# A sum of the hidden halves written to another tile, and the vector engine's work of the down projections held in source order

## The chip, the cores and the metric

The kernel runs on one core of a Trainium2 chip. The metric is the device time of one execution in microseconds (us). It is a single launch, and a profile of one more execution is at hand.

## What is computed

One inference step of a two-layer encoder trunk over 1152 tokens (1024 of a prompt and 8 streams of 16), model width 1024. Each layer is a normalisation, a mixer (stick-breaking attention beside a convolution in layer 0, banded attention in layer 1), a residual, and then the part that matters here:

```python
def rmsnorm(x, g):
    xf = x.astype(jnp.float32)
    r = lax.rsqrt(jnp.mean(xf * xf, axis=-1, keepdims=True) + RMS_EPS)
    return (xf * r).astype(x.dtype) * g

def sq_relu_mlp(h, w_up, w_down):
    return jnp.square(jax.nn.relu(h @ w_up)) @ w_down
...
        xp = xp + op
        xs = xs + os_
        xp = xp + sq_relu_mlp(rmsnorm(xp, norm_ffn[layer]), w_up[layer], w_down[layer])
        xs = xs + sq_relu_mlp(rmsnorm(xs, norm_ffn[layer]), w_up[layer], w_down[layer])
```

`w_up` is 1024x4096 and `w_down` 4096x1024, all in 32-bit floats.

## The kernel before

Every product is computed as three passes over halves: `split` (lines 178 to 181) writes a value's rounded part with ScalarE (`hi`, line 180) and the remainder with VectorE (`lo`, line 181), and TensorE multiplies high by high, high by low and low by high. So each block of weights and each block of activations costs one instruction on ScalarE and one on VectorE before TensorE may read it.

Function `rest` holds the feed-forward part of a layer. Both of its matrix products use a Strassen scheme with seven products in place of eight, so sums and differences of blocks are formed around them.

**Up projection.** `unit(m)` runs 16 times (two of the 32 blocks of 128 hidden channels each time). In a unit, `k` goes over the seven products. `seven` prepares the weights of a product two ahead, `mms` issues 24 matmuls for each product (two column halves `n` of 288 tokens, four chunks, three passes), and `take` empties the PSUM bank with VectorE (lines 1417 to 1429). `done` multiplies by the row scale (line 1394), applies ReLU and square with ScalarE (1395, 1396), forms the three sums t3, t2 and b12 - b11 (1400 to 1402) once the last quarter of its column half is there, and sends the blocks to the DRAM tensor `hb_d` with transfers that GpSimd (POOL) issues (1404, 1406). A bank is used by several products in turn, so a late `take` holds up a later product.

The seventh block of a pair, `last_sum`, is formed one unit later. It is called in `unit(m)` at `k == 2` for unit m - 1 (and once more in the down projection's loop, at item 3). It subtracts t2 from the half (1, 0) of the hidden pair and writes the result over that half (line 1365), which transfer 3 of the same pair reads (line 1406); then it sends the result (1366).

**Down projection.** `todos` lists 112 items (128 in layer 1, where the last product is done in two column halves): for product `k` and block pair `j`, 24 matmuls each (12 in the halved ones), accumulated in eight banks over the 16 pairs of a chain. The loop at line 1597 does for item i: resident weight loads (`resident`), the load of item i + 4 (`load`: the hidden block from `hb_d`, and for products 3, 5 and 6 a weight block through one of three staging buffers of tag `st`), the preparation of item i + 2 (`prep`: `split_b` for activations, in one of four buffers; `split_w` for weights, with sums of weight blocks at lines 1527, 1529, 1530 and 1533), and then `item(i)`. At the end of a chain `item` adds the eight banks to the residual (line 1583). `later` holds what follows a finished quarter (squares, scaled splits, sums of squares), one entry for each item. At item 104 of layer 0, `soon` calls for the first two weight chunks of layer 1's mixer: four more staged loads with a split each, from the same three staging buffers. At the end of unit 15, `begin(0)` calls the loads of items 0 to 3 at `k == 5`, and `begin(1)` their first preparations at `k == 6`.

**What sets the order.** The instructions are not issued in source order as such. A scheduler goes over the whole program with a model of its own for the times, takes on each engine what its model has ready, earlier source lines first, and gives out buffers as they come free. So a VectorE instruction may stand far ahead of its place in the source. `tc.keep_in_program_order(ins)` adds one rule: this instruction is issued on its engine behind the instruction traced just before it on that engine. It adds no wait beyond that order. In the kernel before, it is used for the normalisation's matmuls alone (line 1446).

Of the kernel before, what the change touches and what calls it, by code (L numbers as in the profile page):

```python
# [11 lines left out]
ALU = mybir.AluOpType  # L12
# [21 lines left out]
TW = T // 2  # L34
# [6 lines left out]
def f(ap):  # L41
    return ap.bitcast(F32)
# [77 lines left out]
def tile_trunk(ctx, tc, ins, outs):  # L120
    nc = tc.nc
    ACT = nc.scalar.activation
    tt = nc.vector.tensor_tensor
# [3 lines left out]
    put = nc.gpsimd.dma_start  # L127
# [47 lines left out]
    hb_d = [dram.tile([7, NF // 2, P, TW], F32, name=f"hb_d{l}") for l in range(2)]  # L175


    def split(hi, lo, src):

        ACT(hi, src, AF.Copy)  # L180
        return tt(lo, src, f(hi), ALU.subtract)  # L181
# [168 lines left out]
    class Cat:  # L350
# [5 lines left out]
        def put(self, piece, rows, c0, n):  # L356
            if self.direct is None:
                put(cat_d[self.layer][self.p, rows, c0:c0 + n], piece[rows, :n])
                return
            at = c0  # L360
            while at < c0 + n:
                g = at // G
                m = min(c0 + n, g * G + G) - at
                hi, lo = (x[rows, self.p % 4, at - g * G:at - g * G + m] for x in self.direct[g][self.p // 4])
                split(hi, lo, piece[rows, at - c0:at - c0 + m])
                at += m
# [845 lines left out]
    def rest(layer, ks, cat, rst, mp, then, soon=None):  # L1212
# [12 lines left out]
        def pair(t, n=1024):  # L1225

            return t[:, :n].rearrange("p (a t) -> p a t", a=2)
# [129 lines left out]
        hids = []  # L1357
        tmps = [temps[n // 4][:, n % 4 * TQ:n % 4 * TQ + TQ] for n in range(8)]

        t3, t2 = extra[:, :TW], extra[:, TW:]  # L1360

        def last_sum(m):

            t4 = hids[m % 2 * 2 + 1][:, :TW]
            tt(t4, t4, t2, ALU.subtract)
            put(hb_d[layer][6, m], t4)

        def unit(m):

# [79 lines left out]
                start = 3  # L1449
            for k in range(start, 7):  # L1450
                seven(7 * m + k + 2)
                if m and k == 2:
                    last_sum(m - 1)
                if m == NF // 2 - 1 and k > 4:
                    begin(k - 5)
                for n in range(2):
                    mms(k, n, range(4))
                    if m == 0 and k == 3:
                        nx.rows[n]()
                        if n == 0:  # L1460
                            continue
                        take(k, 0)
                    if m == 0 and (k, n) == (4, 0):
                        nx.rows[2]()
                    take(k, n)
# [11 lines left out]
        a11, a21, a22, braw, bsplit, asplit, streams, bs, ws, later = ({}, {}, {}, [], [], [], {}, {}, {}, [])  # L1477
# [32 lines left out]
        def split_b(i):  # L1510
            while len(bsplit) < 4 and len(bsplit) <= i:
                bsplit.append(pair(own(("th", "xr2", "tm0", "tm1")[len(bsplit)], F32R), T))
            n = bs[i].shape[1]
            t = bsplit[i % 4][:, :, :n]
            split(t[:, 0], t[:, 1], bs[i])
            bs[i] = t

        def split_w(i):
            k, ns, j = todos[i]
            if ns == (1,):  # L1520
                ws[i] = ws[i - 16]
                return
            if k == 3 or k == 6:
                src = streams.pop(i)
            elif k == 5:
                src = streams.pop(i)
                tt(src, src, a22[j], ALU.subtract)
            elif k == 1:
                tt(a21[j], a21[j], a11[j], ALU.subtract)
                tt(a22[j], a22[j], a21[j], ALU.add)  # L1530
                src = a22[j]
            elif k == 2:
                tt(a11[j], a11[j], a22[j], ALU.add)
                src = a11[j]
            else:
                src = a11[j] if k == 0 else a21[j]
            if k == 6 and layer == 1:
                w = pair(place(j // 2, j % 2, F32R, f"wk{name}"))
            elif k == 6:
                if j < 8:  # L1540
                    tag = ("sl8", "sl9", "sl10", "sl11", "lo0", "lo1", "lo2", "xr3")[j]
                    asplit.append(pair(own(tag, F32R)))
                w = asplit[j % 8]
            elif i % 6 < 4:
                w = sp.tile([P, 2, 512], F32R, "hl", f"hl_wd{layer}{i}")
            else:
                w = pair(few[i % 6 - 4])
            split(w[:, 0], w[:, 1], src)
            ws[i] = w

        def prep(i):
            if i < len(todos):
                split_b(i)
                split_w(i)

        def begin(n):

            if n == 0:
                for i in range(4):
                    load(i)  # L1560
            else:
                prep(0)
                prep(1)
# [3 lines left out]
        def item(i):  # L1567
            k, ns, j = todos[i]
            first = any(k == chain[0] for chain in chains) and j == 0
            b, w = bs.pop(i), ws[i]  # L1570
            for m in range(4):
                for n in ns:
                    if first:
                        banks[m, n] = bank(f"pd{layer}{k}{m}{n}")
                    ps = banks[m, n][:, :TQ]
                    for s, (a, h) in enumerate(SPLIT):
                        mm(ps, w[:, a, m * P:m * P + P], b[:, h, (n - ns[0]) * TQ:(n - ns[0]) * TQ + TQ],  # L1577
                           start=first and s == 0, stop=j == NF // 2 - 1 and s == 2,
                           skip_group_check=not any(k == chain[0] for chain in chains))
                    if j == NF // 2 - 1:  # L1580
                        for e, half in out[k]:
                            xs = x[4 * e + m][:, half * TW + n * TQ:half * TW + n * TQ + TQ]
                            tt(xs, xs, ps, ALU.add)
            if j == NF // 2 - 1 and k in final:
                later.extend(then(x, *final[k], None if len(ns) > 1 else ns[0], sq))

# [10 lines left out]
        for i in range(len(todos)):  # L1597
            if i == 3:
                last_sum(NF // 2 - 1)
            if 2 <= i < 18:  # L1600
                resident("a11", i - 2)
            if 14 <= i < 30:
                resident("a21", i - 14)
            if 16 <= i < 32:
                resident("a22", i - 16)
            c = {n: m for m, n in enumerate((6, 7, 8, 9, 40, 41, 42, 43))}.get(i)
            if c is not None:
                x[c] = own(f"sl{c}", F32)
                dma(x[c], xr_d[layer][c])
            load(i + 4)  # L1610
            prep(i + 2)
            item(i)
            if i == 104 and soon:
                soon()
            for _ in range(1 + (len(later) > len(todos) - i)):
                if later:
                    later.pop(0)()
# [220 lines left out]
```

## Time and profile before

| | |
|---|---|
| median of 3 runs (lowest to highest) | 2860.11 us (2855.12 to 2863.78) |
| profiled execution, its own time | 2856.45 us |
| its span, first to last instruction | 2854.7 us |
| mean granted TensorE clock | 0.985 |
| TensorE matmuls (PE) | 2708.8 us busy, 95% |
| VectorE (DVE) | 2141.5 us busy, 75% |
| ScalarE (ACT) | 1376.3 us busy, 48% |
| GpSimd (POOL) | 330.5 us busy, 12% |

Up projections are the matmuls of line 1388, down projections those of line 1577. In a row of the timeline the columns are start, duration, engine, line, operation, what is written <- what is read, size and count; in brackets stands the idle time of the engine before it and what released it. In a row of waits the three numbers are the total in us, how often, and the longest. In a table of windows each engine has its busy time and number of instructions, then come the granted TensorE clock, the share of the DMA engines and GB/s. Names leave buffer numbers out: `um` and `pd` are PSUM banks of the up and the down projection, `hl_wd`, `hl_wc` and the like split weights, `st_wd` and `st_wc` staged ones; `th`, `xr` and `tm` also name the buffers of split activations in the down projection. A busy matmul row counts the modelled, overlapping duration; the pace is read from the starts.

### The profile page before, as it was taken

How to read it: one execution, taken by the hardware profiler on the slowest of the kernel's cores; microseconds unless marked ns; L12 is line 12 of the kernel's file. 1: busy time of each engine (PE TensorE's matmuls, PEld its weight loads, DVE VectorE, ACT ScalarE, POOL GpSimd, SP SyncE). 2: the span in 40 equal slices, each digit the busy share in tenths (PEclk: the TensorE clock that was granted, in tenths of full speed). 3: DMA queues.
4: the chain of work that ended last, by engine and by line, in shares of the span. 5: the costliest groups of instructions: out<-in, count | busy, mean ns of one | idle time of the engine just before them, and what ended most of it. 6: DMA issues, size and time to landing. Idle time of an engine off the chain costs nothing.

```text
span 2854.7 us, 50855 instructions
## 1 busy us (share of the span) xinstructions
PE 2708.8 (95%) x19362; PEld 2594.2 (91%) x19362; DVE 2141.5 (75%) x4201; ACT 1376.3 (48%) x2898; POOL 330.5 (12%) x599
## 2 busy tenths in 40 slices
PE   8988988899999998999999999998999999989998
PEld 8987876799999998999999999997999999989998
DVE  8999999988677768557467777778787676685566
ACT  5344446665444443445355555556554444434343
POOL 1000101031111110000011111110321111100001
PEclk9999998999999999999999999999999999999999
DMA  4434346444333386336444444446543333873354
GB/s 154 131 96 133 107 134 201 147 165 139 128 132 132 137 288 222 109 96 212 139 142 139 143 137 135 136 132 222 173 146 130 124 137 131 283 232 96 93 173 139
DMA packets 177813, 431.31 MB, mean 151 GB/s; under 512 B 26480, under 2 KB 54320, under 8 KB 175520
## 3 DMA queue, kind: packets, MB, share of 16 engines
q1 hardware_dynamic: 140304, 296.77, 33.1%
q0 software_dynamic: 37120, 131.27, 13.5%
q8 instruction: 152, 2.49, 0.4%
q14 instruction: 93, 0.76, 0.1%
q10 hardware_dynamic: 144, 0.02, 0.0%
HBM read 297.98 MB, written 117.34 MB: 145 GB/s over the span
## 4 chain that ended last, share of the span: by engine, by line
PE 51%; DVE 24%; DMA 9%; issue 8%; ACT 7%; POOL 0%; SPq 0%; DVEq 0%; POOLq 0%; ACTq 0%
PE pd L1577 21%; PE psc L220 10%; PE um L1388 6%; DMA hb_d<-hdm 4%; DVE y L669 4%; DVE kp L843 2%; PE avc L401 2%; PE tpc L389 2%; DVE sg L845 1%; PE f L220 1%; PE psoa L220 1%; DVE hdm L1394 1%; DVE hl_m L181 1%; DMA st_wd<-in_w_down_dram 1%; DVE wla L181 1%
## 5 line engine op out<-in xcount | busy, mean ns | idle before, releaser
L220 PE MATMUL psc<-h,hl_wc 128*128 128x384 f32 x1728 | 327.2, 339 | 0.0
L220 PEld LDWEIGHTS psc<-h,hl_wc 128*128 128x128 f32 x1728 | 296.9, 188 | 13.3 <-issue 10.9
L1388 PE MATMUL um<-sl,hl_m 128*128 128x288 f32 x1548 | 244.7, 299 | 11.2 <-DVE hdm L1423 10.0
L1388 PEld LDWEIGHTS um<-sl,hl_m 128*128 128x128 f32 x1548 | 219.7, 190 | 14.6 <-ACT hdm L1396 8.2
L1577 PE MATMUL pd<-tm,hl_wd 128*128 128x288 f32 x1536 | 210.4, 295 | 4.9 <-DVE tm L181 3.9
L1577 PEld LDWEIGHTS pd<-tm,hl_wd 128*128 128x128 f32 x1536 | 205.2, 189 | 6.8 <-DVE tm L181 5.0
L669 DVE SCALAR_TENSOR_TENSOR y<-u,dw,y 128x1024 f32<-128x1024 f32 (+1 forms) x232 | 176.5, 809 | 0.4
L220 PE MATMUL psp<-h,hl_wi 128*128 128x384 f32 x864 | 168.3, 343 | 0.2 <-ACT kps L892 0.2
L220 PEld LDWEIGHTS psp<-h,hl_wi 128*128 128x128 f32 x864 | 149.2, 190 | 6.4 <-issue 4.9
L1395 ACT ACTIVATE hdm<-hdm 128x288 f32<-128x288 f32 x192 | 84.3, 439 | 138.8 <-DVE hdm L1394 138.8
L180 ACT ACTIVATE hl_m<-xr 128x512 fp32r<-128x512 f32 x132 | 81.0, 622 | 136.2 <-DVE xr L1338 117.7
L1388 PE MATMUL um<-sl,hl 128*128 128x288 f32 x756 | 124.3, 304 | 15.4 <-DVE hdm L1423 15.0
L181 DVE TENSOR_TENSOR tm<-xr,tm 128x576 fp32r<-128x576 f32 (+1 forms) x120 | 85.3, 714 | 70.0 <-ACT tm L180 70.0
L180 ACT ACTIVATE tm<-xr 128x576 fp32r<-128x576 f32 (+1 forms) x120 | 77.6, 647 | 119.2 <-PE pd L1577 98.2
L1388 PEld LDWEIGHTS um<-sl,hl 128*128 128x128 f32 x756 | 109.9, 194 | 18.7 <-DVE hdm L1423 16.9
L181 DVE TENSOR_TENSOR hl_m<-xr,hl_m 128x512 fp32r<-128x512 f32 x132 | 92.3, 700 | 44.7 <-ACT hl_m L180 44.7
L1104 ACT ACTIVATE s<-s,mxc 128x640 f32<-128x640 f32 (+4 forms) x128 | 88.9, 694 | 60.1 <-DVE mxc L1101 58.5
L1577 PE MATMUL pd<-th,hl_wd 128*128 128x288 f32 x768 | 107.8, 295 | 2.3 <-DVE hdm L1429 2.2
L1577 PE MATMUL pd<-tm,hl 128*128 128x288 f32 x768 | 105.9, 295 | 1.2 <-DVE tm L181 1.2
L1577 PE MATMUL pd<-xr,hl_wd 128*128 128x288 f32 x768 | 106.9, 295 | 0.0
L1577 PEld LDWEIGHTS pd<-th,hl_wd 128*128 128x128 f32 x768 | 103.5, 189 | 3.2 <-DVE hdm L1429 2.7
L1577 PEld LDWEIGHTS pd<-tm,hl 128*128 128x128 f32 x768 | 103.3, 188 | 2.1 <-DVE tm L181 2.1
(527 smaller groups left out, 6809.6 us busy)
## 6 DMA issues: line engine op xcount, KB each, us to landing
xr<-hb_d SPq DMA_DIRECT2D x208, 288.0 KB, 2.9
hb_d<-hdm POOLq DMA_DIRECT2D x128, 288.0 KB, 3.0
xr<-in_w_up_dram SPq DMA_DIRECT2D x64, 512.0 KB, 4.4
st_wd<-in_w_down_dram SPq DMA_DIRECT2D x96, 256.0 KB, 3.5
hb_d<-t POOLq DMA_DIRECT2D x64, 288.0 KB, 2.4
wm<-in_w_down_dram SPq DMA_DIRECT2D x64, 256.0 KB, 4.7
st_wc<-in_w_in_c_dram SPq DMA_DIRECT2D x48, 256.0 KB, 2.9
xm_d<-xo POOLq DMA_DIRECT2D x16, 576.0 KB, 3.5
```

The source lines that it names most:

```text
L180: ACT(hi, src, AF.Copy)
L181: return tt(lo, src, f(hi), ALU.subtract)
L220: mm(ps()[:, :G], hl[:, a, at:at + P], act[g][k // 4][b][:, k % 4, :], start=n == 0, stop=n == len(todo) - 1)
L389: nc.tensor.transpose(tp[:, c0 + q * P:c0 + (q + 1) * P], blocks.get(j, tile_q), ident)
L401: mm(st["av"][:, o0:o0 + n], vs[:, j, i].rearrange("p a d -> p (a d)"), src[:, c0:c0 + n], start=st["done"] == 0, stop=st["done"] == nmm - 1)
L669: stt(src if j == CW - 1 else dst, src, wj, dst, ALU.mult, ALU.add)
L843: nc.vector.tensor_tensor_scan(keep[:, 0:n][:, ::-1], keep[:, 0:n][:, ::-1], ones[:, 0:1].to_broadcast([P, n]), 1.0, ALU.mult, ALU.mult)
L845: tt(w[:, 0:n - 1], w[:, 0:n - 1], keep[:, 1:n], ALU.mult)
L1104: ACT(s[:, :n], s[:, :n], AF.Exp, bias=mx, scale=-1.0, accum_out=tot)
L1388: mm(banks[b, n][:, :TQ], w[:, a, c * P:c * P + P], combo(key, c)[:, h, n * TQ:n * TQ + TQ], start=k < 3 and c == 0 and i == 0, stop=c == ...
L1395: ACT(y, y, AF.Relu)
L1577: mm(ps, w[:, a, m * P:m * P + P], b[:, h, (n - ns[0]) * TQ:(n - ns[0]) * TQ + TQ], start=first and s == 0, stop=j == NF // 2 - 1 and s == ...
```

## The change

It has two parts. First, `last_sum` writes its result to t3 in place of the hidden half itself, the transfer reads t3, and the call stands at `k == 1` of the next unit, with the instruction kept in source order. Second, in the down projections every VectorE instruction that belongs to an item (the splits of `split_b` and `split_w`, the sums of weight blocks, the additions to the residual) is kept in source order, and the difference a21 - a11 (line 1529) leaves `split_w` and is done at items 18 to 33, between `prep(i + 2)` and `item(i)`. The VectorE instructions of `later`, of `soon` and of the up projection's `take` and `done` are not marked.

```diff
         t3, t2 = extra[:, :TW], extra[:, TW:]
+        pinned = tc.keep_in_program_order
 
         def last_sum(m):
 
-            t4 = hids[m % 2 * 2 + 1][:, :TW]
-            tt(t4, t4, t2, ALU.subtract)
-            put(hb_d[layer][6, m], t4)
+            pinned(tt(t3, hids[m % 2 * 2 + 1][:, :TW], t2, ALU.subtract))
+            put(hb_d[layer][6, m], t3)
...
                 seven(7 * m + k + 2)
-                if m and k == 2:
+                if m and k == 1:
                     last_sum(m - 1)
...
             t = bsplit[i % 4][:, :, :n]
-            split(t[:, 0], t[:, 1], bs[i])
+            pinned(split(t[:, 0], t[:, 1], bs[i]))
             bs[i] = t
...
             elif k == 5:
                 src = streams.pop(i)
-                tt(src, src, a22[j], ALU.subtract)
+                pinned(tt(src, src, a22[j], ALU.subtract))
             elif k == 1:
-                tt(a21[j], a21[j], a11[j], ALU.subtract)
-                tt(a22[j], a22[j], a21[j], ALU.add)
+                pinned(tt(a22[j], a22[j], a21[j], ALU.add))
                 src = a22[j]
             elif k == 2:
-                tt(a11[j], a11[j], a22[j], ALU.add)
+                pinned(tt(a11[j], a11[j], a22[j], ALU.add))
                 src = a11[j]
...
-            split(w[:, 0], w[:, 1], src)
+            pinned(split(w[:, 0], w[:, 1], src))
             ws[i] = w
...
-                            tt(xs, xs, ps, ALU.add)
+                            pinned(tt(xs, xs, ps, ALU.add))
...
             load(i + 4)
             prep(i + 2)
+            if 18 <= i < 34:
+                pinned(tt(a21[i - 18], a21[i - 18], a11[i - 18], ALU.subtract))
             item(i)
```

## Prediction

> **What bounds the kernel now.** I read the page first, then the waits of VectorE and TensorE, then windows of the two stages that the change touches, then timelines inside them.
>
> ```profile
> span 2854.7 us, 50855 instructions
> PE 2708.8 (95%) x19362; PEld 2594.2 (91%) x19362; DVE 2141.5 (75%) x4201; ACT 1376.3 (48%) x2898; POOL 330.5 (12%) x599
> DVE hdm L1365 <- DMA hb_d<-hdm: 100.1, 32, 5.9
> PE um L1388 <- DVE hdm L1423: 25.1, 17, 2.3
> PE pd L1577 <- DVE sl L1583: 13.9, 3, 6.1
> PE pd L1577 <- DVE tm L181: 5.0, 7, 1.2
> 676.00:1031.80 355.80, 341.30 (x2529) 337.72 (x2528) 252.56 (x494) 164.88 (x375) 56.90 (x105) 1.00 0.41 144
> 2111.00:2464.70 353.70, 341.57 (x2519) 339.22 (x2518) 250.88 (x490) 164.06 (x373) 56.85 (x105) 0.99 0.42 144
> 1363.33 3.36 PE L1577 MATMUL pd<-th,lo 128*128 128x288 f32 x24
> 1366.53 3.36 PE L1577 MATMUL pd<-xr,lo 128*128 128x288 f32 x24
> ```
>
> TensorE bounds the kernel; only its holes can be won. Undisturbed it starts 24 matmuls of 288 columns in 1366.53 - 1363.33 = 3.20 us, 0.1333 each. The two windows hold the up projections without their first units: 2529 and 2519 matmuls would take 337.2 and 335.9 us, so 18.6 + 17.8 = 36.4 us are lost there. VectorE is not the bound by its share, but it stands still 32 times, once in each unit, 3.1 us on average, in front of the last sum (L1365) until a transfer has read the half that the sum overwrites. One unit shows how that reaches TensorE:
>
> ```profile
> 752.79 0.54 POOL L1406 DMA_DIRECT2D hb_d<-hdm  x1 [1.66 <-ACT tm L1415]
> 759.52 0.76 DVE L1365 TENSOR_TENSOR hdm<-hdm,t 128x576 f32<-128x576 f32 x1 [5.90 <-DMA hb_d<-hdm]
> 767.00 2.53 PE L1388 MATMUL um<-sl,hl 128*128 128x288 f32 x9 [2.25 <-DVE hdm L1423]
> 733.10 0.76 DVE L1365 TENSOR_TENSOR hdm<-hdm,t 128x576 f32<-128x576 f32 x1 [2.20 <-DMA hb_d<-hdm]
> 741.01 1.22 PEld L1388 LDWEIGHTS um<-sl,hl_m 128*128 128x128 f32 x9 [0.34 <-ACT hdm L1396]
> ```
>
> Where VectorE stood 5.90 us, the bank for product 6 came 2.25 us late; where it stood 2.20 us, TensorE lost about 0.3 us. A unit of 168 matmuls has 22.4 us. The first window holds 2529 / 168 = 15.1 units with 252.56 us of VectorE, 16.8 for each, so without the stand it has room; with it, and with short waits for ScalarE's half of each split, it has little.
>
> **Part one: the last sum into t3.** The overwritten operand was the only reason to wait for transfer 3. Nothing is added: one instruction of 0.76 us and one transfer stay. The new place adds one wait: t3 must have been read by its own transfer (L1404). That is issued 4.4 us before transfer 3 (748.42 against 752.79); the landings are those of the t2 and t3 transfers in layer 0.
>
> ```profile
> 748.42 0.54 POOL L1404 DMA_DIRECT2D hb_d<-t  x1 [3.90 <-DVE t L1400]
> 752.07 0.43 ACT L1396 ACTIVATE hdm<-hdm 128x288 f32<-128x288 f32 x1
> DMA to landing us min/median/max: 2.4/2.4/4.5
> ```
>
> Even at the longest landing (4.5 us) t3 is free at 752.9, 0.4 us after the square that the sum needs. The next writer of t3 is L1400 one unit later, some 17 us after the new transfer's issue: no wait there. POOL's later transfers move forward with the sum. The pin puts it behind a weight split that has run long before, and so holds nothing. Ends: all 36.4 us (TensorE gapless), or half, 18, if the scheduler still leaves it in a poor place. I take 33, near the upper end, since the unit with a stand of 2.2 us already lost almost nothing.
>
> Of those losses a part is clock: after the hole at 764.9 to 767.0 the granted clock is 0.50.
>
> ```profile
> 767.50:770.00 2.50, 2.50 (x12) 2.50 (x12) 1.78 (x4) 2.17 (x5) 0.00 (x0) 0.50 0.31 118
> 1094.50:1098.00 3.50, 3.42 (x15) 3.45 (x16) 3.50 (x9) 0.00 (x0) 0.00 (x0) 0.52 0.90 284
> ```
>
> The Trainium skill ("TensorE: Matmul & The Clock Gate", Part 1) has the clock halved only after an idle window of about 3.4 us. By that, holes of at most 2.3 us cost their 25.1 us alone, the rest of the 36.4 has another cause and stays, and the forecast comes out 8 us longer, 2824. This trace does not agree: 2.25 us were enough, so I give that no chance of its own.
>
> **Part two: down projections in source order.** What the order of the scheduler costs now:
>
> ```profile
> 1093.39 0.68 DVE L1530 TENSOR_TENSOR lo<-lo,wm 128x512 f32<-128x512 f32 x1
> 1093.99 3.00 DVE L1583 TENSOR_TENSOR sl<-sl,pd 128x288 f32<-128x288 f32 x8
> 1094.58 4.88 PE L1577 MATMUL pd<-th,hl 128*128 128x288 f32 x24 [6.13 <-DVE sl L1583]
> ```
>
> At the first chain's end VectorE forms sums of weights (L1530 here) that are due 16 items later, and empties the banks after them. Pinned, the eight additions (3.00 / 8 = 0.375 us each) follow each bank's end, every 0.40 us, and the next item finds its banks. That takes away the 13.9 us of waits for L1583 (one of 6.1 in each layer and a third), and 3.5 x 0.48 = 1.7 us of half clock after each long one: 17. The waits for L181 (5.0 us) have the same cause except at the start: 4. The sums, undone there, fall into items 16 to 47: neighbours overlap by 0.08 us (0.68 long, 0.60 apart, at 1093.39), so VectorE has then 0.67 + 0.61 for the two splits and 0.61 for a sum, 1.9 us per item, 2.5 where a second sum falls, against 3.20: covered by TensorE.
>
> The pins cost something at three joins, where unpinned work stands ahead of them.
>
> The first is the start. Items 0 and 1 are now prepared behind L1402 of unit 15; before, weight 0 was split at 1025.54.
>
> ```profile
> 1025.54 0.69 DVE L181 TENSOR_TENSOR hl_wd<-st_wd,hl_wd 128x512 fp32r<-128x512 f32 x1 [1.15 <-ACT hl_wd L180]
> 1030.08 0.45 DVE L1426 TENSOR_TENSOR hdm<-um,tm 128x288 f32<-128x288 f32 x1
> 1032.65 0.75 DVE L1400 TENSOR_TENSOR t<-hdm,hdm 128x576 f32<-128x576 f32 x1
> 1034.35 0.75 DVE L1402 TENSOR_TENSOR hdm<-hdm 128x576 f32<-128x576 f32 x1
> 1035.53 0.67 PE L1577 MATMUL pd<-th,hl_wd 128*128 128x288 f32 x3 [0.77 <-DVE hdm L1429]
> 1043.40 0.40 PE L1577 MATMUL pd<-tm,hl_wd 128*128 128x288 f32 x1 [0.78 <-ACT tm L180]
> ```
>
> From L1426 to L1402's end are 5.0 us, 4.0 without the weight split (0.69) and the addition (0.45) that stood between; item 0's two splits add 1.4. Product 6's 24 matmuls cover 3.2 of these 5.4 to 6.4 us: TensorE waits 2.2 to 3.2, and half clock may add 1.5. The two holes shown (1.55 us) go. Net 0.6 to 3.2 a layer; I take 1.5, so 3.
>
> The second is `soon` in layer 0. Its four splits are not pinned, but item 107's split is pinned behind the last of them.
>
> ```profile
> 1361.58 0.33 SPq L187 DMA_DIRECT2D st_wc<-in_w_in_c_dram  x1
> 1368.21 0.93 SPq L187 DMA_DIRECT2D st_wc<-in_w_in_c_dram  x2
> 1370.09 2.36 SPq L187 DMA_DIRECT2D st_wd<-in_w_down_dram  x2
> 1367.49 0.69 DVE L181 TENSOR_TENSOR hl_wc<-st_wc,hl_wc 128x512 fp32r<-128x512 f32 x1 [2.07 <-ACT hl_wc L180]
> 1371.40 0.69 DVE L181 TENSOR_TENSOR hl_wc<-st_wc,hl_wc 128x512 fp32r<-128x512 f32 x1 [1.34 <-ACT hl_wc L180]
> ```
>
> SP's order shows staging buffers given out in source order: the four st_wc, then items 109 and on. Now items 107 and 108 hold two of the three buffers until their splits, which wait for the four; so the four pass one after another through one buffer. One pass, issue to split's end, is 1372.09 - 1368.21 = 3.9 us, or 1368.18 - 1361.58 = 6.6 at worst. It begins when item 106 is split, about 2.2 us after item 103 starts (then its activation buffer comes free; two VectorE splits of 1.4 behind one of ScalarE). With 4.5 a pass: 2.2 + 18 + 1.4 = 21.6 us, where four items cover 12.8. TensorE stands 8.8 us (6.4 to 17.2 by the ends). SP's loads for 109 on wait too, but land before they are due. I take 9.
>
> The third is layer 1's last product, 16 items of 12 matmuls. Its weight splits ran ahead; pinned, they fall into it.
>
> ```profile
> 2786.86 0.69 DVE L181 TENSOR_TENSOR wkm<-st_wd,wkm 128x512 fp32r<-128x512 f32 x1 [1.22 <-ACT wkm L180]
> 2790.38 0.75 DVE L1657 TENSOR_TENSOR accfin<-accfin,t 128x576 f32<-128x576 f32 x1
> 2797.79 0.62 DVE L276 TENSOR_SCALAR accfin<-ident,v_fin 96x96 f32<-96x96 f32 x3
> 2803.73 2.28 DVE L1719 SCALAR_TENSOR_TENSOR sl<-sl,norms,rfin 128x576 f32<-128x576 f32 x3
> ```
>
> An item has 12 x 0.1333 = 1.6 us. VectorE, by starts: 15 pairs of splits (0.61 and, for half an activation, 0.37) 14.7; four sums of squares at 0.67, 2.7; two normalisations at 1.2 (the diagonal, 0.62, and five small steps, put as long) 2.4; eight scalings at 2.28 / 3 = 0.76, 6.1. That is 25.9 us against 15 items' 24.0. I take 2, between 0 (TensorE's own extra work covers it) and 6 (waits of the in-order queue come on top).
>
> **Sum.** Against the profiled execution's own 2856.45 (0.13% under the median 2860.11): -33 - 17 - 4 + 3 + 9 + 2 = -40, so 2816. Less than 0.3%, 8.6 us, can't be told from no change.
>
> **Rivals.** (a) *The joins cost nothing* (buffers are given out otherwise, the first splits float): -54, 2802. SP's order above speaks against it. (b) *The last sum still waits*, now for t3's transfer or in a poor place: 18 in place of 33, 2831. The maximum landing of 4.5 us speaks for a wait of 0.4 at most. (c) *Slower: the staging loop.* With splits pinned, a staging buffer is freed only at its item's turn, and the loop of three buffers (landing, two splits of 1.4, up to one item of waiting) must stay under three items, 9.6 us. At the median landing it is 3.5 + 1.4 + 3.2 = 8.1.
>
> ```profile
> DMA to landing us min/median/max: 2.5/3.5/9.2
> ```
>
> At a mean landing over 5.0 it binds; the 96 streamed items must slip 0.5 us each, a landing of 6.5, to take back the 40 and cost 8.6 more: 2865. (d) *No change*: the holes only move, since TensorE's next limit lies right behind; 2856; against it stand the 16.8 us of VectorE in a unit of 22.4.
>
> **Numbers.** Forecast 0.52, (a) 0.20, (b) 0.13, (c) 0.08, (d) 0.07. Faster by over 0.3%: the first three, 0.85; the same 0.07; slower 0.08. The range runs from (a) with all of the 36.4, 2799, to (b) with the second join at its worse end, 2839, and 3 us beyond either, as runs of one kernel spread (2855.12 to 2863.78): 2796 to 2842. It leaves out (c) and (d).
>
> **What would show it.** L1365 with under 1 us of idle time before it; PE's waits for L1423 nearly gone and the two windows near 338 us; no wait of 6 us for L1583; new PE holes at the first down matmul (2 to 3 us), at item 107 of layer 0 (9 us) and small ones after item 98 of layer 1. The forecast is wrong if the mixer between, whose order the scheduler makes anew, shifts by more than some us, or if VectorE is seen waiting for st_wd at its pins.

## The result, and the profile after

The changed kernel took 2830.38 us (median of 4 runs, 2823.68 to 2831.08) beside 2857.61 us for the kernel before on the same chip (2850.0 to 2863.78): a ratio of 0.9901, with a 95% interval of 0.9871 to 0.993. That is inside the range given. The profiled execution took 2830.25 us, 26.2 under the 2856.45 of before, where the forecast had 40.

Line numbers below the last sum's own shift a little between the kernels. In the changed one, the down projection's matmul is line 1576 (1577 before), the addition to the residual line 1582 (1583 before), and the difference a21 - a11 of the down weights line 1612; the up projection's matmul stays at 1388 and the last sum at 1365.

A ledger by stage says more than the total. Each stage is taken from the first matmul of its line to the first matmul of the next stage's line (the down projections to their own last matmul's end), in us of each kernel's profiled execution. The last column is the ratio to the kernel before, from the timed runs.

| kernel | up, layer 0 | down, layer 0 | up, layer 1 | down, layer 1 | span | ratio |
|---|---|---|---|---|---|---|
| before | 387.4 | 370.1 | 385.3 | 378.0 | 2854.7 | 1 |
| changed | 378.1 | 369.4 | 375.9 | 369.9 | 2828.5 | 0.9901 |
| part one alone (`e1_sum_alone`) | 375.2 | 371.6 | 373.6 | 376.3 | 2832.1 | 0.9927 |
| part two alone (`e2_pins_alone`) | 385.0 | 370.6 | 383.2 | 369.6 | 2839.8 | 0.9963 |
| `e7_dest_only` | 374.8 | 372.0 | 374.8 | 376.4 | 2832.4 | 0.9937 |
| `e8_in_place` | 382.9 | 370.4 | 383.7 | 369.9 | 2840.7 | 0.9975 |
| `e3_late_soon` | 373.6 | 360.1 | 375.0 | 369.3 | 2809.8 | 0.9865 |
| `e4_late_s1` | 365.9 | 368.7 | 366.1 | 368.8 | 2807.0 | 0.9827 |
| `e5_both` | 364.6 | 360.6 | 366.1 | 370.8 | 2798.9 | 0.9807 |
| `e6_fewer_pins` | 378.2 | 357.1 | 373.5 | 360.5 | 2802.8 | 0.9834 |
| `e10_additions_only` | 376.7 | 370.4 | 372.2 | 374.6 | 2826.9 | 0.9941 |
| `e11_weight_sums` | 376.6 | 359.0 | 374.9 | 360.5 | 2805.5 | 0.9824 |
| `e9_best` | 364.6 | 356.6 | 365.6 | 359.6 | 2779.0 | 0.9759 |

The mixer between the layers took 675.7 to 678.5 us in all of them, and what lies ahead of the first up projection 642.8 to 647.9: the time moved in the four stages named. Between kernels that have the same source in a stage it differs by up to 4.6 us (the up projections of the changed kernel, of `e3_late_soon`, `e6_fewer_pins`, `e10_additions_only` and `e11_weight_sums`), so a difference of a few us in one stage is not argued from without a row that shows it. The spans are those of one execution each; in `e8_in_place` and `e10_additions_only` it was the shortest of the timed ones, 4.4 and 7.2 us under their medians.

Of the changed kernel, the page's head, its waits, and the windows of the up projections, which end at the first down matmul as the ones before did and are as long within 1.2 us:

```profile
span 2828.5 us, 50713 instructions
PE 2705.3 (96%) x19362; PEld 2592.1 (92%) x19362; DVE 2146.1 (76%) x4201; ACT 1380.5 (49%) x2898; POOL 329.5 (12%) x599
DVE s1m L1336 <- DMA xr<-in_w_up_dram: 79.4, 28, 4.2
PE um L1388 <- DVE hdm L1423: 12.6, 18, 1.3
PE pd L1576 <- DVE tm L181: 6.6, 3, 5.8
667.00:1022.70 355.70, 348.12 (x2597) 345.16 (x2596) 261.04 (x507) 174.12 (x395) 57.77 (x107) 1.00 0.43 150
2094.00:2446.50 352.50, 347.44 (x2594) 344.90 (x2594) 261.14 (x507) 174.16 (x395) 57.78 (x107) 1.00 0.43 150
```

Three things are to be seen. VectorE's stand of 100.1 us before the last sum has left the list, and a new one of 79.4 us is at its head: L1336, the sum s1 of two blocks of the *up* weights, waits 28 times (2.8 us each) for the load of those weights. TensorE's waits for L1423 are halved, not gone. In about the same time TensorE starts 2597 and 2594 matmuls where it started 2529 and 2519; at the prediction's 0.1333 us the windows still lose 355.7 - 346.2 = 9.5 and 352.5 - 345.8 = 6.7 us.

What L1365 itself now waits for, in the view of that one line:

```profile
  ACT hdm L1396: 13.3, 18
  DMA hb_d<-t: 3.0, 2
```

That is 16.3 us in 32 calls, 0.5 each, as the prediction asked for (under 1 us). But this is what became of the room, in the timeline of one unit:

```profile
750.60 2.42 SPq L1323 DMA_DIRECT2D xr<-in_w_up_dram  x2
752.58 0.75 DVE L1365 TENSOR_TENSOR t<-hdm,t 128x576 f32<-128x576 f32 x1
754.70 0.69 DVE L1338 TENSOR_TENSOR xr<-s1m,xr 128x512 f32<-128x512 f32 x1
759.10 0.69 DVE L1336 TENSOR_TENSOR s1m<-xr 128x512 f32<-128x512 f32 x1 [3.33 <-DMA xr<-in_w_up_dram]
764.48 1.45 PE L1388 MATMUL um<-sl,hl 128*128 128x288 f32 x9 [0.20 <-DVE hdm L1423]
```

The last sum runs at 752.58 without a stand, and 2.4 us after its end VectorE stands all the same, 3.33 us, in front of s1. Each unit forms s1 (L1336), then a21 - a11 (L1337), then a11 (L1338) from it. Product 2 of this unit starts at 751.4, so the L1338 at 754.70 is already the next unit's, and the s1 at 759.10 that of the unit after: the scheduler has put it more than a unit (22 us) ahead of its place in the source. VectorE comes to it at 755.77, 3.1 us after the second of its two loads was issued (753.02 less 0.33), and the load lands 3.33 us later.

In the down projections the profile has both sides of part two. The waits for L1583 are gone. At `soon` in layer 0, the timelines of SP, VectorE and TensorE:

```profile
1358.08 12.39 SPq L187 DMA_DIRECT2D st_wc<-in_w_in_c_dram  x4
1373.96 0.33 SPq L187 DMA_DIRECT2D st_wd<-in_w_down_dram  x1
1361.68 0.69 DVE L181 TENSOR_TENSOR hl_wc<-st_wc,hl_wc 128x512 fp32r<-128x512 f32 x1 [3.63 <-ACT hl_wc L180]
1365.49 0.69 DVE L181 TENSOR_TENSOR hl_wc<-st_wc,hl_wc 128x512 fp32r<-128x512 f32 x1 [3.12 <-ACT hl_wc L180]
1369.42 0.69 DVE L181 TENSOR_TENSOR hl_wc<-st_wc,hl_wc 128x512 fp32r<-128x512 f32 x1 [3.24 <-ACT hl_wc L180]
1373.23 0.69 DVE L181 TENSOR_TENSOR hl_wc<-st_wc,hl_wc 128x512 fp32r<-128x512 f32 x1 [3.12 <-ACT hl_wc L180]
1364.40 4.42 PE L1576 MATMUL pd<-tm,sl 128*128 128x288 f32 x32
1374.65 4.33 PE L1576 MATMUL pd<-tm,sl 128*128 128x288 f32 x16 [5.82 <-DVE tm L181]
1378.78 3.75 PE L1576 MATMUL pd<-th,lo 128*128 128x288 f32 x24
1374.70:1378.20 3.50, 3.50 (x14) 3.40 (x15) 3.01 (x5) 0.63 (x1) 0.00 (x0) 0.50 0.81 246
```

The four mixer chunks pass one after another through one staging buffer: of their four loads each but the first is issued within 0.03 us of the end of the split before it (as that of st_wd at 1373.96, behind the last), a split every 3.8 to 3.9 us, and TensorE stands at item 107. The 32 matmuls from 1364.40 end about 1368.67, so 5.98 us are lost; the next 16 take 4.13 us in place of 2.13, at a granted clock of 0.50, and the 24 after them 3.59 in place of 3.20. Together 8.4 us.

### The profile page after: what moved, and what is told of

It reads as the page before. It is cut to its first block, busy times and chain, and to the rows that moved or that the text cites. A ratio compares the mean times of both kernels' runs of the same rounds, so it can differ in the third digit from the quotient of the medians.

```text
span 2828.5 us, 50713 instructions
## 1 busy us (share of the span) xinstructions
PE 2705.3 (96%) x19362; PEld 2592.1 (92%) x19362; DVE 2146.1 (76%) x4201; ACT 1380.5 (49%) x2898; POOL 329.5 (12%) x599
## 4 chain that ended last, share of the span: by engine, by line
PE 51%; DVE 24%; DMA 10%; ACT 8%; issue 6%; SPq 0%; POOL 0%; DVEq 0%; ACTq 0%; POOLq 0%
PE pd L1576 19%; PE psc L220 10%; PE um L1388 9%; DMA xr<-in_w_up_dram 4%; DVE y L669 4%; DMA st_wd<-in_w_down_dram 3%; DVE kp L843 3%; PE avc L401 2%; DVE hl_m L181 2%; PE tpc L389 2%; DVE sg L845 1%; PE psoa L220 1%; PE f L220 1%; DMA wm<-in_w_down_dram 1%; DVE wla L181 1%
## 5 line engine op out<-in xcount | busy, mean ns | idle before, releaser
L1576 PEld LDWEIGHTS pd<-xr,hl_wd 128*128 128x128 f32 x768 | 103.7, 189 | 1.2 <-DVE hl_wd L181 0.8
```

## The experiments

**Each part alone.** The kernel before with part one, and the changed kernel with the last sum as it was:

```diff
 # e1_sum_alone, against before
+        pinned = tc.keep_in_program_order
...
-            tt(t4, t4, t2, ALU.subtract)
-            put(hb_d[layer][6, m], t4)
+            pinned(tt(t3, hids[m % 2 * 2 + 1][:, :TW], t2, ALU.subtract))
+            put(hb_d[layer][6, m], t3)
...
-                if m and k == 2:
+                if m and k == 1:
 # e2_pins_alone, against the changed kernel: the same lines, all but the first, the other way round
```

> The first part alone: the last sum goes to t3, one product earlier in the source and kept in source order; the down projections are as before. Theory (the two parts act in different stages and add): the two up projections come from 387.6 and 385.5 us to 378 and 376, the down projections stay at 370 and 378, the whole is 17 to 20 us shorter than before, 2838 beside 2857. Rival (the parts need each other: a shorter up projection only brings the down projections' stalls forward): less than 10 us shorter. Either way VectorE stands still in front of the sum of weight blocks s1 until the up weights have landed, some 2.8 us a unit.

Measured: 2833.8 us, ratio 0.9927 (0.9912 to 0.9942), 19.6 us under the 2853.36 of the kernel before.

> The second part alone: the down projections' VectorE work in source order, the last sum as before. Theory: the up projections stay at 386 to 388 us with 3.1 us of waiting a unit for the transfer; in the down projections the two holes of 6 us at the first chain's end go, and a hole of 6 us at item 107 of layer 0 comes, so that they take 369 and 370 us: 8 to 10 us shorter than before, 2848. Rival: the hole at the first chain's end goes only if the up projection ends in the new order; then the down projections stay at 370 and 378.

Measured: 2841.82 us, ratio 0.9963 (0.9952 to 0.9974), 11.5 us under. The waits of VectorE in the two, and of TensorE in the second:

```profile
DVE s1m L1336 <- DMA xr<-in_w_up_dram: 80.7, 28, 4.8
```

```profile
DVE hdm L1366 <- DMA hb_d<-hdm: 106.4, 32, 6.2
PE um L1389 <- DVE hdm L1424: 24.6, 19, 2.3
PE pd L1577 <- DVE th L181: 5.8, 2, 2.9
```

Part one brings its gain in the up projections and the new stand with it, without part two. Part two brings its gain in the second down projection (378.0 to 369.6; the first stays at 370, with one hole gone and one new) and leaves TensorE's waits for the emptied banks (24.6 us) where they were. The parts add up (19.6 + 11.5 = 31 against 1 - 0.9901 of 2857.6, which is 28, with 20 to 37 in its interval), and the larger is part one's. The last row is a surprise that is needed below: with the old last sum in the last unit, the first item waits 2.9 us a layer for its split; in the changed kernel it is 1.05 in both layers.

**What of part one does it: the destination, the place or the pin?**

```diff
 # e7_dest_only, against before: t3 as the destination, no pin, still after product 2
-            t4 = hids[m % 2 * 2 + 1][:, :TW]
-            tt(t4, t4, t2, ALU.subtract)
-            put(hb_d[layer][6, m], t4)
+            tt(t3, hids[m % 2 * 2 + 1][:, :TW], t2, ALU.subtract)
+            put(hb_d[layer][6, m], t3)
 # e8_in_place, against the changed kernel: pin and place kept, written over the operand
-            pinned(tt(t3, hids[m % 2 * 2 + 1][:, :TW], t2, ALU.subtract))
-            put(hb_d[layer][6, m], t3)
+            t4 = hids[m % 2 * 2 + 1][:, :TW]
+            pinned(tt(t4, t4, t2, ALU.subtract))
+            put(hb_d[layer][6, m], t4)
```

> The kernel before with one edit: the last sum is written to t3 and t3 is what the transfer reads; it stands after product 2 as before and is not pinned. Theory: the destination does it all, since the overwritten operand was the only reason to wait: no stand before L1365, up projections 374 to 376 us each as with the whole first part (375.2 and 373.6), ratio 0.992 to 0.994, about 2834 us. Rival: the place and the pin matter: unpinned, the scheduler puts the sum where the splits wait behind it, the up projections keep half of the loss (380 to 382 each), about 2845 us.

Measured: 2834.01 us, ratio 0.9937 (0.9918 to 0.9955); up projections 374.8 and 374.8.

> The changed kernel, but the last sum overwrites its operand as before and sends that; it stays pinned after product 1. Theory: the wait for the transfer that reads the operand is back and, since the sum comes one product earlier, longer than before: VectorE stands 100 to 150 us before L1365, the up projections take 385 to 400 us each, the down projections as in the changed kernel; 2840 to 2870 us. Rival: the pin alone brings the gain, because the order of VectorE is what counted: VectorE stands under 60 us, up projections under 382 each, about 2835 us.

Measured: 2846.86 us, ratio 0.9975 (0.9963 to 0.9987); up projections 382.9 and 383.7. VectorE's first wait:

```profile
DVE hdm L1366 <- DMA hb_d<-hdm: 106.8, 32, 5.4
```

The destination does all of part one. With it alone the up projections are as short as with the whole part, and without it pin and place leave the stand at 106.8 us. Nor do they bring anything: `e2_pins_alone` is the same kernel without them and has a ratio of 0.9963, lower than the 0.9975 here. That the earlier place would make the stand much longer was expected and did not come: 106.8 us are as much as the 106.4 of `e2_pins_alone`, and the number for the up projections (385 to 400) was too high.

**The new wait.** In the changed kernel, the two sums at the head of a unit's weights are called at a place of their own and pinned there: product 4 of the unit before.

```diff
 # e4_late_s1, against the changed kernel
+        early_s1 = {}
+
+        def sums(m, pin=lambda ins: ins):
+            a1, a2 = raws[m]
+            s1 = early_s1[m] = sp.tile([P, 512], F32, "st", f"s1{name}{m}")
+            pin(tt(s1, a2[:, :512], a2[:, 512:], ALU.add))
+            pin(tt(a2[:, :512], a2[:, :512], a1[:, :512], ALU.subtract))
...
-                tt(s1, a21, a22, ALU.add)
-                tt(a21, a21, a11, ALU.subtract)
+                if m not in early_s1:
+                    sums(m)
+                s1 = ups["s1"] = early_s1[m]
...
+                if 0 < m < NF // 2 - 1 and k == 4:
+                    sums(m + 1, pinned)
```

> The changed kernel with the two sums of up-weight blocks that wait for a landing (s1 and a21 - a11) called at product 4 of the unit before, each kept in source order, so that they stand behind the additions that empty product 3's banks. Theory (VectorE's wait for the up weights has taken the place of the wait removed, and holds up the additions behind it): the 79 us of waits for the up weights go, the 12.6 us of TensorE's waits for the emptying of product 4's bank too, and the up projections come to 369 to 371 us each, 12 to 16 us in all under the changed kernel. Rival (VectorE's work in a row between products 2 and 4 is itself too long): the waits for the load go, the holes at product 6 stay at 0.7 us or more, and the gain is under 4 us.

Measured: 2806.44 us, ratio 0.9827 (0.9807 to 0.9847). VectorE's longest sum of waits, then what s1 (L1330 here) waits for in all, and one unit of the timeline (L1346 is L1338 of the other kernels):

```profile
DVE tm L181 <- ACT tm L180: 80.6, 52, 4.9
  DMA xr<-in_w_up_dram: 2.3, 2
751.70 0.68 DVE L1330 TENSOR_TENSOR s1m<-xr 128x512 f32<-128x512 f32 x1
754.11 0.69 DVE L1346 TENSOR_TENSOR xr<-s1m,xr 128x512 f32<-128x512 f32 x1
```

The sum now stands 2.4 us ahead of the one that uses it, not a unit ahead, and its 79.4 us of waiting are 2.3. It does not stand where the expectation put it, behind product 3's additions: its pin holds it behind a weight split that itself runs ahead, and it comes between the additions of product 1.

The up projections fall by another 12.2 and 9.8 us, more than expected (369 to 371 was; 365.9 and 366.1 came), and TensorE has no wait left there for an emptied bank. So the stand before s1 held back what part one could give: with it gone, the up projections are 40.7 us shorter than before, with it 18.7. (That is the least of the seven kernels that have the new destination and the old s1; the other six have 21.0 to 24.1.)

**The hole at item 107.** `soon` is called at the last item of the down projection:

```diff
 # e3_late_soon, against the changed kernel
-            if i == 104 and soon:
+            if i == len(todos) - 1 and soon:
```

> The changed kernel with the first two weight chunks of the next mixer called for at the last item of the down projection of layer 0 in place of item 104, so that none of this stage's pinned work stands behind their splits. Theory (the four splits stand ahead of item 107 and pass one after another through one staging buffer): the hole of 5.8 us at item 107 goes, the down projection of layer 0 takes 361 to 363 us in place of 369.4, the mixer after it starts without a new wait over 1 us, and the whole is 6 to 8 us shorter than the changed kernel. Rival (the hole comes from the loads' landing, not from the order): the chunks are now late at the mixer's start and the hole moves there, no gain.

Measured: 2815.46 us, ratio 0.9865 (0.985 to 0.9879). The hole is gone, the first down projection 360.1 us (369.4), and nothing came in its place in the mixer. Its first up projection, which the edit doesn't touch, also came out 4.5 us shorter; with the other repair beside it (next run) no such difference shows.

```diff
 # e5_both, against the changed kernel: the edits of e4_late_s1 and e3_late_soon
```

> The changed kernel with both repairs at once: the sums s1 and a21 - a11 called and pinned at product 4 of the unit before, and `soon` called at the last item. Alone, by their profiles, the first left the up projections at 365.9 and 366.1 us (378.1 and 375.9 in the changed kernel) and the second the down projections of layer 0 at 360.1 (369.4). Theory: the two holes lie in different stages and add: up projections 365 to 367 each, first down projections 359 to 362, TensorE shows neither a wait of about 6 us before item 107 nor waits of VectorE for the up weights; ratio to the kernel before 0.979 to 0.981, about 2796 to 2800 us. Rival: the gain of the late `soon` was half a gift of the scheduler's other order (its up projections were also 4.5 us shorter in layer 0), then the two don't add and the ratio stays at 0.982 or above.

Measured: 2798.42 us, ratio 0.9807 (0.9787 to 0.9828). The two holes add, as two different stages should.

**Which pins does part two need?** Three kernels keep one kind or two of the pins of the down projections:

```diff
 # e6_fewer_pins, against the changed kernel: the splits free, sums and additions pinned
-            pinned(split(t[:, 0], t[:, 1], bs[i]))
+            split(t[:, 0], t[:, 1], bs[i])
...
-            pinned(split(w[:, 0], w[:, 1], src))
+            split(w[:, 0], w[:, 1], src)
 # e10_additions_only, against e6_fewer_pins: the sums of lines 1527 to 1532 and 1612 free too, for instance
-                pinned(tt(a21[i - 18], a21[i - 18], a11[i - 18], ALU.subtract))
+                tt(a21[i - 18], a21[i - 18], a11[i - 18], ALU.subtract)
 # e11_weight_sums, against e6_fewer_pins: the additions free, the sums pinned
-                            pinned(tt(xs, xs, ps, ALU.add))
+                            tt(xs, xs, ps, ALU.add)
```

> The changed kernel without the pins of the weight splits and the activation splits; the sums of the weights and the eight residual additions stay pinned. Theory: the gain of part two comes from the additions and the sums alone, and the splits pay the price: with them free the four splits of `soon` need not pass through one buffer, so the hole before item 107 of layer 0 and the small waits for VectorE's splits in the staging loop go; first down projections 361 to 364 us (369.4 in the changed kernel), the second 367 to 369, 6 to 9 us under the changed kernel, ratio about 0.987. Rival: the splits need their pins; free, they are put behind other work again, TensorE's waits for L181 come back (5 us or more in all), and the time is that of the changed kernel or up to 5 us above.

Measured: 2803.32 us, ratio 0.9834 (0.9806 to 0.9862). Better than expected: both down projections gain (12.3 and 9.4 us), and TensorE is busy in all but 0.2 us of the first:

```profile
1024.00:1381.00 357.00, 356.80 (x2691) 356.59 (x2691) 233.55 (x378) 156.64 (x254) 10.23 (x19) 1.00 0.57 182
```

> The changed kernel with only the eight residual additions of each product pinned in the down projections; the sums of the weights and the splits are not. Theory: the wait of about 6 us was the order of the additions behind sums that are due much later, so pinning the additions alone takes it away: no wait of TensorE for L1582 over 1 us, down projections 357 to 362 us each, the time of the kernel without pinned splits, ratio 0.982 to 0.985. Rival: free sums are still put ahead of the additions at the first chain's end, since a pinned addition keeps its place behind them only if they were called later; then the waits of about 6 us stay, down projections 366 to 372 each, ratio 0.988 to 0.992.

Measured: 2835.88 us, ratio 0.9941 (0.9922 to 0.9961). The theory fell; the rival's mechanism came, at a ratio above its 0.988 to 0.992. The wait is back, and VectorE's timeline before it shows why:

```profile
PE pd L1576 <- DVE sl L1582: 14.1, 3, 6.8
1080.57 0.68 DVE L1612 TENSOR_TENSOR wm<-wm,wm 128x512 f32<-128x512 f32 x1
1081.17 1.29 DVE L1529 TENSOR_TENSOR lo<-lo,wm 128x512 f32<-128x512 f32 x2
1082.38 3.00 DVE L1582 TENSOR_TENSOR sl<-sl,pd 128x288 f32<-128x288 f32 x8
1082.97 3.46 PE L1576 MATMUL pd<-th,hl 128*128 128x288 f32 x13 [6.80 <-DVE sl L1582]
```

Line 1612 is called from item 18 on, and yet it runs ahead of the additions that close item 15: the pin of an addition keeps it behind the instruction traced before it, and keeps nothing from being put in front of the pair. The one to hold is the instruction that runs ahead.

> The changed kernel with only the sums of the weight blocks pinned in the down projections; the splits and the eight residual additions of each product are not. With only the additions pinned the down projections took 370.4 and 374.6 us and the wait of 6 to 7 us for L1582 stayed; with both pinned they took 357.1 and 360.5. Theory: the sums held at their own items are the whole of part two's gain, since nothing else stands ahead of the additions: no wait for L1582 over 1 us, down projections 356 to 362 us each, ratio 0.982 to 0.985. Rival: the additions need their pins as well, since a free addition can be put behind the splits of the next items: waits for L1582 of 1 to 6 us, down projections 364 to 372 each, ratio 0.986 or above.

Measured: 2807.06 us, ratio 0.9824 (0.98 to 0.9847); down projections 359.0 and 360.5. The sums' pins, with a21 - a11 at its new place, are the whole gain: the new place without the pins is `e10_additions_only`, and the pins without the new place were not run. The additions need none, and the pins of the splits only cost.

**The version that the runs point to:** the sums of the up weights late (`e4_late_s1`) and no pin on the splits (`e6_fewer_pins`).

```diff
 # e9_best, against the changed kernel: the edits of e4_late_s1 and e6_fewer_pins
```

> The changed kernel with the sums s1 and a21 - a11 called and pinned at product 4 of the unit before, and without the pins of the splits. Alone the first left the up projections at 365.9 and 366.1 us, the second the down projections at 357.1 and 360.5. Theory: the two act in different stages and add: up projections 365 to 367 each, down projections 357 to 361 each, about 20 us under the first repair alone: 2784 to 2790 us, ratio 0.975 to 0.978. Rival: the free splits of the down projections' first items now compete with the sums pinned in the last unit, and the start of each down projection loses 2 to 5 us: ratio 0.979 or above.

Measured: 2784.18 us, ratio 0.9759 (0.9739 to 0.9779), 70 us under the kernel before in the same call (2854.34) and far below the changed one. The windows of its four stages:

```profile
643.30:1007.90 364.60, 362.32 (x2714) 360.27 (x2713) 292.57 (x564) 193.27 (x417) 62.05 (x111) 1.00 0.44 155
1007.90:1364.60 356.70, 356.70 (x2693) 356.70 (x2691) 234.04 (x378) 157.39 (x254) 10.29 (x20) 1.00 0.56 181
2041.80:2407.40 365.60, 362.55 (x2714) 360.27 (x2713) 293.35 (x564) 193.25 (x417) 62.70 (x112) 1.00 0.44 154
2407.40:2767.00 359.60, 359.60 (x2720) 359.26 (x2719) 238.40 (x422) 153.99 (x267) 11.28 (x21) 1.00 0.53 170
```

TensorE is busy from end to end of both down projections and lacks 2 to 3 us in each up projection. Little is left to be won there by order.

## Why the prediction was right, and where its sum was not

The mechanism of both parts was as forecast: the stand before the last sum was the overwritten operand's (`e7_dest_only`, `e8_in_place`), and the waits for L1583 came from sums of weights put ahead of the additions (`e10_additions_only`, `e11_weight_sums`). The sizes, term by term:

**Last sum and up projections: -33 forecast, -18.7 measured.** This is the term that was mis-sized, and its 14.3 us are about as much as the 13.8 between forecast and profiled execution. Its lower end (18) is what came, though not for the reason given there: the last sum's own place cost nothing (0.5 us of waiting a unit). The step that failed is "so without the stand it has room". It counted VectorE's work but did not ask what is late next. The next was the load of the up weights: in the kernel before, the stand had covered it (s1 waited 2.0 us there, in 2 calls), so no large row of that profile warned of it; the loads and s1 stood in the same timelines and could have been set against each other, once the last sum's stand was thought away.

The prediction's own two windows, taken from and to the same matmuls, show the size. They lasted 355.8 and 353.6 us before, 345.6 and 341.1 in the changed kernel (22.7 less), and 335.6 and 334.0 in `e4_late_s1` (39.8 less), so the new wait held back 17.1. The stretches ahead of them, which the prediction left out, grew by 3.9 us in the changed kernel; in `e3_late_soon`, with the same source, they did not. That the 39.8 are above the upper end of 36.4 is a matter of pace: in `e4_late_s1` every unit after the first takes 22.3 to 22.4 us, 0.1327 a matmul and not 0.1333, and there were some 5050 of them.

**Down projections: -21 for the waits, +14 for the joins, -7 in all; measured -8.7** (the rounded stages of the ledger give 8.8). Split by items, both layers together, in us against the kernel before; `e6_fewer_pins` has the pins that work without those that cost:

| items | forecast | changed | `e6_fewer_pins` |
|---|---|---|---|
| 0 to 12, with the start | +3 | -2.8 | -8.3 |
| 13 to 16, the first chain's end | -21 | -17.0 | -21.0 |
| 17 to 95 | 0 | -1.4 | -1.4 |
| the rest of layer 0, with `soon` | +9 | +8.4 | +0.1 |
| the rest of layer 1 | +2 | +4.2 | +0.3 |

The -21 for the waits was right in size: with the splits free it came whole. The pins of the splits cost 21.7 us (the difference of the last two columns), not 14: some 5.5 at the start, 4.0 at items 13 to 16, which the forecast put at nothing, 8.3 with `soon` and 3.9 at the end of layer 1. The start came out shorter all the same, because the kernel before lost 8.3 us there (6.5 against `e11_weight_sums`, whose splits are free too), where the prediction took off two holes of 1.55 us a layer. The net agrees partly by luck, since a start that was 5.8 us better than forecast pays for what the chain's end and layer 1's end cost more.

- *Join 2, `soon`: +9 forecast, 8.4 in the profile.* The place, the item, the buffer and the pass (3.8 to 3.9 us; 4.5 taken) were as forecast; the clock at 0.50 behind the hole was not in the sum and made up for the shorter passes, so the agreement to 0.6 us is in part luck. Moving `soon` took out 9.3 us of the stage.
- *Join 1, the start: +1.5 a layer forecast, a gain measured.* In the changed kernel, in layer 0:

```profile
1022.71 1.10 PE L1576 MATMUL pd<-th,hl_wd 128*128 128x288 f32 x7
1023.39 0.75 DVE L1402 TENSOR_TENSOR hdm<-hdm 128x576 f32<-128x576 f32 x1
1024.05 0.75 DVE L181 TENSOR_TENSOR th<-xr,th 128x576 fp32r<-128x576 f32 x1
1024.86 2.13 PE L1576 MATMUL pd<-th,hl_wd 128*128 128x288 f32 x14 [1.05 <-DVE th L181]
1024.90:1027.90 3.00, 3.00 (x23) 3.00 (x23) 2.96 (x6) 0.82 (x2) 0.53 (x1) 1.00 1.05 400
```

  VectorE's order is the one forecast (the split behind L1402), but TensorE starts item 0 on the high halves, which need no VectorE, and so covers 0.93 us more; the hole of 1.05 us leaves the clock at 1.00, so the 1.5 us of half clock did not come. In the kernel before, items 0 to 2 took 1043.40 - 1031.80 = 11.6 us for 9.6 us of matmuls; here they take 11.1. Two steps failed: an item was taken to need all of its halves before it starts, and the last unit's own stand was left in although part one takes it away. With that stand (`e2_pins_alone`; 4.74 us in the last unit of layer 0, and another 1.76 in which VectorE waits there for a late square of ScalarE) the hole is 2.9 us behind the same 0.93, so the forecast's 2.2 to 3.2 would have been near by two errors.
- *Join 3, the end of layer 1, +2 forecast, +4.2 measured:* waits for splits show there, under 1 us each, 1.6 us in all, while the 1.7 us that the kernel before waited there for L1583 are gone. The rest of the 4.2 was not traced.
- *Put at nothing:* small holes at items 13 to 15, the last of the first product with streamed weights, 2.0 us a layer more than in `e6_fewer_pins`. VectorE's pinned split waits 2.4 to 3.2 us there for ScalarE's, which waits for the staged load, and the load is issued as the split before it ends (1063.25 behind 1063.22). That is rival (c), the staging loop, right in kind and far off in size. It is also the last sign that the prediction named against itself, VectorE waiting for st_wd at its pins, by way of ScalarE.

**The rivals.** Of (b), half of the up projections' loss stayed and the time was 2830 against its 2831, but not by its mechanism; a time that agrees proves no cause. Of (a), the condition was that the first splits float; `e6_fewer_pins` made it true and came to 2803 against its 2802, by other terms: -21.0 in the up projections for -33, and -30.4 in the down projections for -21.

## What to carry to other kernels

Before a wait is priced as a gain, think it away in the timeline and look for the next thing that the same engine will meet; a wait that now covers another leaves it hardly a row. Pin the instruction that runs ahead (here, sums due many items later), not what it delays and not the splits around it: a pinned instruction behind an unpinned transfer waits for that transfer's buffer too. And read a change by stage, and a stage by items: a net that agrees can be terms that are off both ways.

## What was not expected of the hardware

The length of a hole does not tell what TensorE's clock does behind it. In the kernel before, the four longest holes of the up projections are 2.23 to 2.25 us long. Behind two of them, those that end at 767.00 and 2223.53, the granted clock is 0.50; behind the other two, at 910.73 and 2341.99, it stays at 1.00. The holes of 2.91 and 2.90 us at the start of the second down projection part the same way: half clock in `e2_pins_alone` (hole's end at 2461.82), full in `e8_in_place` (2462.96). Windows of 3.41 us around the holes at 767.00 and 910.73, then around these two:

```profile
763.34:766.75 3.41, 1.41 (x11) 1.18 (x9) 2.27 (x6) 2.18 (x5) 0.00 (x0) 1.00 0.00 0
766.75:770.16 3.41, 3.16 (x13) 3.16 (x14) 2.66 (x6) 2.19 (x5) 0.68 (x2) 0.50 0.22 87
906.70:910.11 3.41, 1.80 (x14) 1.56 (x12) 2.27 (x5) 1.90 (x5) 0.00 (x0) 1.00 0.00 0
910.11:913.52 3.41, 2.79 (x21) 2.79 (x22) 2.66 (x7) 2.47 (x6) 0.54 (x1) 1.00 0.22 87
```

```profile
2458.29:2461.70 3.41, 0.61 (x5) 0.38 (x3) 3.07 (x6) 1.76 (x4) 1.09 (x2) 1.00 1.04 407
2461.70:2465.11 3.41, 3.29 (x14) 3.30 (x15) 3.38 (x8) 1.02 (x2) 0.54 (x1) 0.50 1.06 412
2458.04:2461.45 3.41, 2.02 (x16) 1.78 (x14) 1.68 (x3) 2.73 (x7) 0.94 (x2) 1.00 1.05 401
2461.45:2464.86 3.41, 1.90 (x14) 1.90 (x15) 3.41 (x7) 0.40 (x1) 1.08 (x2) 1.00 1.05 408
```

The windows are cut where the trace's record of the granted clock can change: in the thirteen profiles every stretch at 0.50, but for each profile's last, is one, two or three times 3.41 us long (90, 60 and 16 of them). In the first case of each pair the hole lies almost whole in one such step, in the second it is shared by two. In the up and down projections after the first 35 us of each up projection, where a full step has 25 or 26 starts of a matmul, a step at full clock with at most 10 starts was followed by half clock in 22 of 22 cases, one with 11 in 3 of 7, and one with 12 or more in none. So by these rows a hole of 2.25 us costs, as an estimate, 1.7 us more than itself (half of 3.41) or nothing, by where it falls; and the prediction's "2.25 us were enough" holds for the hole that it looked at. The Trainium skill ("TensorE: Matmul & The Clock Gate", Part 1) puts the halving behind an idle window of about 3.4 us that runs free of the kernel, and the way back behind a busy one of the same length. These traces agree on the window's length and that it takes no heed of the kernel; they differ in that the window need not be idle, since one with 10 of its 26 matmuls was enough.
